# Putting the prior, the loads and the stores of a mixture-of-softmaxes kernel into one hardware queue

## The chip, the cores and the metric

The kernel runs on one core of a Trainium2 chip. The metric is the device time of one execution in microseconds (us), here always the median of several runs. A run of one core has no second die to compare with, so a run counts as slow only if it is over 1.5% above the fastest of its kernel.

## The reference

```python
logits: (32, 128, 4, 4096) float32      prior: (32, 128, 4) float32
prior_probs = softmax(prior, axis=-1)
softmax     = softmax(logits, axis=-1)
mixture     = sum over the 4 heads of prior_probs[..., None] * softmax     # (32, 128, 4096)
```

There are 4096 rows of 4 heads of 4096 values: 268.4 MB in and 67.1 MB out.

## The kernel before

A tile is 128 rows (one in each partition) with all four heads, 8.39 MB, and there are 32 tiles. Two tile buffers take the loads, two output buffers the results. For each tile ScalarE makes four exps with their sums, VectorE the reciprocals, GpSimd the four weights (the "weight multiply"), and VectorE adds up the four weighted heads in four steps. A helper, `only`, gives each instruction exactly the waits that are listed.

```python
def load(u):                       # all loads on SyncE's queue
    ...                            # cuts: whole tiles, halves for the first and the last three
    ld = nc.sync.dma_start(out=ltile[:, u % 2, h:to], in_=lg[u // J, u % J, :, h:to, :])
    if u >= 2:
        only(ld, adds[u - 2, 0] if h == 0 else exps[u - 2, to - 1])
    ...

def store(u, acc, eng, lo=0, hi=V):
    st = eng.dma_start(out=ov[u // J, u % J, :, lo:hi], in_=acc[:, lo:hi])
    stores[u] = only(st, adds[u, H - 1])
...
    load(0)
    nc.scalar.dma_start(out=pr, in_=pv)          # the prior, ScalarE's queue
    load(1)
...
        for h in range(H):
            late = h == H - 1 and 4 <= u < U - 3
            if h == H - 1 and 0 < u < U - 3:
                store(u - 1, obuf[:, (u - 1) % 2], nc.scalar)     # stores 0 to 27
            exp(h, *((stores[u - 4],) if late else ()))
            ...
        if u + 2 < U:
            load(u + 2)
        if u == U - 3:                                            # stores 28 to 31: SyncE
            store(u - 1, obuf[:, (u - 1) % 2], nc.sync)
            store(u, acc, nc.sync)
```

`late` is one more wait of a tile's fourth exp, for store u-4; the list of waits of this kernel shows no time lost to it. At the end of the build one function moves the first half of load 0 ahead of the start barrier.

The softmax here doesn't subtract the row's maximum and nothing guards it: scores larger than these inputs give would overflow.

## Time and profile before

| | before |
|---|---|
| device time | 781.02 us |
| span | 779.3 us |
| busy: VectorE, ScalarE | 67%, 60% |
| transfer engines' time, SyncE's queue + ScalarE's queue | 82.3% + 17.6% |
| moved | 335.66 MB, 431 GB/s |
| steady distance from one tile's landing to the next | 24.18 us |

The last row is taken from the starts of the first exp of each tile, which waits for the load: tile 14 at 354.86, tile 27 at 669.25, 13 tiles. The transfer engines are busy all the time, so the reading is about them. The page's table of issues tells the time from issue to landing:

```profile
out_dram<-obuf ACTq DMA_DIRECT2D x28, 2048.0 KB, 29.4
ltile<-in_logits_dram SPq DMA_DIRECT2D x28, 30.9
pr<-in_prior_dram ACTq DMA_DIRECT2D x1, 64.0 KB, 7.0
```

Its columns are tile and tensor, issuing engine, count, size (left out for the whole tiles), and the median time to landing in us. With no load beside them, stores 29 and 30 landed 4.83 and 4.85 us after the store before; beside a load a store takes 29.4, because the two take turns row by row.

### The profile page before, as it was taken

Reading aid. Unit: us, or ns where it says so; the run is one execution under the profiler, and the core shown is the slowest. Engines: PE = TensorE matmul, PEld = TensorE weight load, DVE = VectorE, ACT = ScalarE, POOL = GpSimd, SP = SyncE. Lnnn points to the kernel's source line nnn. Section 1 sums busy time; section 2 is a strip of 40 time slices with the busy share of each in tenths; the row PEclk is TensorE's granted clock in tenths of the full one; section 3 lists DMA queues with packets and bytes.
Section 4 is the critical chain, followed back from the end, with each engine's and each line's share of the span. In section 5 each row is a group of like instructions: output and inputs, shape, how many; then the busy total and the mean of one; then the engine's idle time right before and its main releaser. Section 6 shows DMA issues by size and latency. Waiting matters only on the chain.

```text
span 779.3 us, 654 instructions
## 1 busy us (share of the span) xinstructions
DVE 521.0 (67%) x174; ACT 466.7 (60%) x258; POOL 8.3 (1%) x41
## 2 busy tenths in 40 slices
DVE  4447875558755587555775557855578655689886
ACT  4476555775457755577555675546765567657782
POOL 0000000000000000000000000000000000000000
DMA  9999999999999999999999999999999999999998
GB/s 407 457 417 401 470 407 434 428 461 428 405 467 403 458 420 433 442 443 418 431 454 407 454 408 467 420 415 447 432 442 417 463 399 463 410 427 433 434 429 377
DMA packets 10117, 335.66 MB, mean 431 GB/s; under 512 B 1136, under 2 KB 1136, under 8 KB 1152
## 3 DMA queue, kind: packets, MB, share of 16 engines
q1 hardware_dynamic: 6048, 276.83, 82.3%
q10 hardware_dynamic: 4064, 58.79, 17.6%
q14 instruction: 5, 0.04, 0.0%
HBM read 268.50 MB, written 67.11 MB: 431 GB/s over the span
## 4 chain that ended last, share of the span: by engine, by line
DMA 64%; ACT 27%; DVE 6%; issue 2%; POOL 0%; DVEq 0%; POOLq 0%
DMA ltile<-in_logits_dram 62%; ACT ebuf L159 19%; ACT ltile L159 8%; DVE obuf L177 5%; DMA out_dram<-obuf 2%; DVE ltile L183 1%; POOL coeff L170 0%; DVE rden L168 0%; DVEq L240 0%; POOLq L240 0%; POOLq L170 0%
## 5 line engine op out<-in xcount | busy, mean ns | idle before, releaser
L183 DVE SCALAR_TENSOR_TENSOR obuf<-ebuf,coeff,obuf 128x4096 f32<-128x4096 f32 x90 | 403.6, 4484 | 3.8 <-POOL coeff L170 0.6
L159 ACT ACTIVATE ebuf<-ltile 128x4096 f32<-128x4096 f32 x90 | 322.9, 3589 | 7.4 <-DMA ltile<-in_logits_dram 7.4
L159 ACT ACTIVATE ltile<-ltile 128x4096 f32<-128x4096 f32 x38 | 137.3, 3614 | 280.6 <-DMA ltile<-in_logits_dram 280.6
L168 DVE RECIPROCAL rden<-dsum 128x4 f32<-128x4 f32 (+1 forms) x36 | 6.3, 175 | 227.9 <-ACT ebuf L159 225.1
L177 DVE TENSOR_SCALAR obuf<-ltile,coeff 128x4096 f32<-128x4096 f32 x30 | 70.6, 2353 | 10.2 <-POOL coeff L170 10.2
L183 DVE SCALAR_TENSOR_TENSOR ltile<-ltile,coeff 128x4096 f32<-128x4096 f32 (+1 forms) x7 | 27.0, 3875 | 0.8 <-POOL coeff L170 0.6
L159 ACT ACTIVATION_READ_ACCUMULATOR ebuf<-ltile 128x1 f32 x90 | 16.8, 186 | 0.0
L170 POOL TENSOR_TENSOR coeff<-rden,pp 128x4 f32<-128x4 f32 (+1 forms) x36 | 7.2, 200 | 755.3 <-DVE rden L168 745.4
L159 ACT ACTIVATION_READ_ACCUMULATOR ltile<-ltile 128x1 f32 x38 | 7.1, 186 | 0.0
L139 DVE TENSOR_REDUCE pmax<-pr 16x256 f32<-16x1024 f32 x1 | 1.2, 1208 | 7.8 <-DMA pr<-in_prior_dram 7.8
L141 ACT ACTIVATE pr<-pr 16x1024 f32<-16x1024 f32 x1 | 1.1, 1055 | 7.8 <-DVE pr L140 7.8
L177 DVE TENSOR_SCALAR ltile<-ltile,coeff 128x4096 f32<-128x4096 f32 x2 | 4.7, 2354 | 0.6 <-POOL coeff L170 0.6
L144 DVE TENSOR_TENSOR pn<-pr,pmax 16x1024 f32<-16x1024 f32 x1 | 1.9, 1939 | 0.1
L141 ACT ACT_TABLE_LOAD x1 | 1.3, 1283 | 1.2 <-PEq L229 1.2
L142 DVE TENSOR_REDUCE pmax<-pr 16x256 f32<-16x1024 f32 x1 | 1.2, 1207 | 1.1 <-ACT pr L141 1.1
L149 DVE STREAM_TRANSPOSE pp<-pn 32x256 f32<-32x256 f32 x4 | 1.7, 435 | 0.1
L143 DVE RECIPROCAL pmax<-pmax 16x256 f32<-16x256 f32 x1 | 1.7, 1741 | 0.0
L140 DVE TENSOR_TENSOR pr<-pr,pmax 16x1024 f32<-16x1024 f32 x1 | 1.2, 1211 | 0.0
L138 POOL MEMSET pn<- 32x1024 f32 x1 | 0.9, 941 | 0.3 <-POOLq L229 0.3
L229 POOL MEMSET const-bfloat16-1.0<- 128x1 bf16 x1 | 0.1, 106 | 0.0
L229 POOL MEMSET const-uint8-127<- 128x1 uint8 x1 | 0.1, 106 | 0.0
L229 POOL MEMSET const-float32-0.0<- 128x1 f32 x1 | 0.1, 103 | 0.2 <-issue 0.2
(1 smaller groups left out, 0.1 us busy)
## 6 DMA issues: line engine op xcount, KB each, us to landing
out_dram<-obuf ACTq DMA_DIRECT2D x28, 2048.0 KB, 29.4
ltile<-in_logits_dram SPq DMA_DIRECT2D x7, 4096.0 KB, 26.1
ltile<-in_logits_dram SPq DMA_DIRECT2D x2, 2048.0 KB, 30.9
out_dram<-obuf SPq DMA_DIRECT2D x2, 2048.0 KB, 33.9
out_dram<-ltile SPq DMA_DIRECT2D x1, 2048.0 KB, 17.2
out_dram<-ltile SPq DMA_DIRECT2D x2, 1024.0 KB, 4.8
ltile<-in_logits_dram SPq DMA_DIRECT2D x28, 30.9
pr<-in_prior_dram ACTq DMA_DIRECT2D x1, 64.0 KB, 7.0
```

Source lines behind the costliest of these rows:

```text
L139: nc.vector.reduce_max(pmax, pr, axis=AX.X)
L140: nc.vector.tensor_sub(pr, pr, pmax.unsqueeze(2).to_broadcast([G, R, H]))
L141: nc.scalar.activation(pr, pr, AF.Exp)
L142: nc.vector.reduce_sum(pmax, pr, axis=AX.X)
L143: nc.vector.reciprocal(pmax, pmax)
L144: nc.vector.tensor_mul(pn[0:G].rearrange("g h r -> g r h"), pr, pmax.unsqueeze(2).to_broadcast([G, R, H]))
L149: nc.vector.transpose(pp[32 * t : 32 * (t + 1)], pq[:, :, :, 32 * t : 32 * (t + 1)])
L159: ex = nc.scalar.activation(es[h], lt[:, h], AF.Exp, accum_out=dsum[:, u, h : h + 1])
L168: rc = nc.vector.reciprocal(rden[:, u, h : h + n], dsum[:, u, h : h + n])
L170: mul = nc.gpsimd.tensor_mul(coeff[:, u, h : h + n], rden[:, u, h : h + n], ppu[:, h : h + n])
L177: st = nc.vector.tensor_scalar(out=acc[:, lo:hi], in0=es[h][:, lo:hi], scalar1=coeff[:, u, h : h + 1], scalar2=None, op0=ALU.mult,)
L183: st = nc.vector.scalar_tensor_tensor(out=acc[:, lo:hi], in0=es[h][:, lo:hi], scalar=coeff[:, u, h : h + 1], in1=acc[:, lo:hi], op0=ALU.mu ...
```

## The change

The intent is one queue for everything: the prior first, then the loads, each store between two loads, and no issuing work on ScalarE. The core of the diff:

```diff
-def early_first_load(nc):
+def early_transfers(nc):
+    # (cut) moves the first TWO transfers of SyncE ahead of the barrier: the prior, half of load 0
...
+        nc.sync.dma_start(out=pr, in_=pv)
         load(0)
-        nc.scalar.dma_start(out=pr, in_=pv)
         load(1)
...
-                late = h == H - 1 and 4 <= u < U - 3
                 if h == H - 1 and 0 < u < U - 3:
-                    store(u - 1, obuf[:, (u - 1) % 2], nc.scalar)
-                exp(h, *((stores[u - 4],) if late else ()))
+                    store(u - 1, obuf[:, (u - 1) % 2], nc.sync)
+                exp(h)
```

More of the change, by code (lines that the diff above doesn't have):

```diff
@@ L11, with of_sp @@
 AX = mybir.AxisListType
-def early_first_load(nc):
+def early_transfers(nc):
     blocks = nc.main_func.blocks
-    first = next(
-        (b, i)
-        for b in blocks[1:]
-        for i in b.instructions
-        if i.engine == mybir.EngineType.SP and i.opcode == "DMACopy"
-    )
-    block, ins = first
-    assert not ins.sync_info.on_wait
-    block.instructions.remove(ins)
-    at = next(
-        n
-        for n, i in enumerate(blocks[0].instructions)
-        if i.engine == mybir.EngineType.SP and i.opcode == "Drain"
-    )
-    blocks[0].instructions.insert(at, ins)
+    def of_sp(block, opcode):
+        return [
+            i
+            for i in block.instructions
+            if i.engine == mybir.EngineType.SP and i.opcode == opcode
+        ]
+    body = next(b for b in blocks[1:] if of_sp(b, "DMACopy"))
+    for ins in of_sp(body, "DMACopy")[:2]:
+        assert not ins.sync_info.on_wait
+        body.instructions.remove(ins)
+        drain = of_sp(blocks[0], "Drain")[0]
+        blocks[0].instructions.insert(blocks[0].instructions.index(drain), ins)
 @with_exitstack
@@ L46 @@
     nc = tc.nc
-    nc.at_finalize(early_first_load)
+    nc.at_finalize(early_transfers)
     B, S, H, V = logits.shape
```

## The prediction

> **What bounds the kernel now.** I read the page's busy shares first, then its transfer rows, then the chain of waits, then stretches of the run one by one. The busy shares and the transfer rows:
>
> ```profile
> DVE 521.0 (67%) x174; ACT 466.7 (60%) x258; POOL 8.3 (1%) x41
> ...
> DMA  9999999999999999999999999999999999999998
> ...
> DMA packets 10117, 335.66 MB, mean 431 GB/s; under 512 B 1136, under 2 KB 1136, under 8 KB 1152
> ...
> q1 hardware_dynamic: 6048, 276.83, 82.3%
> q10 hardware_dynamic: 4064, 58.79, 17.6%
> ```
>
> No compute engine is above 67%, and the transfer engines are at 9 tenths in every slice but the last. The two hardware queues (q1 is SyncE's, q10 ScalarE's) add up to 99.9% of the 16 engines' time. So the kernel is bound by transfers: 268.4 MB of logits in, 67.1 MB out, at 431 GB/s over 779.3 us. No wait could be removed to gain much, unless the engines themselves moved bytes faster. The stretches between landings tell whether they can (columns: length, busy us of DVE, ACT, POOL with counts, granted clock, transfer share, GB/s):
>
> ```profile
> 22.39:41.73 19.34, 11.58 (x5) 7.30 (x4) 0.20 (x1) 1.00 1.00 434
> 112.34:693.42 581.08, 383.60 (x121) 348.14 (x193) 4.82 (x24) 1.00 1.00 433
> ```
>
> The first stretch lies between the landings of tiles 0 and 1. Only one queue works then (the whole-window transfer view shows q1 alone, at 100.2%), and one tile of 8.389 MB takes 19.34 us, 434 GB/s. The second is 24 steady tiles, each a load of 8.389 MB and a store of 2.097 MB on two queues: 581.08 / 24 = 24.21 us a tile, 433 GB/s. One queue of pure loads is as fast as two queues of mixed traffic. Pure stores on one queue are seen at the end: stores 28, 29 and 30 were issued on q1 at 727.84, 736.98 and 756.35 and took 36.0, 31.7 and 17.2 us to land, so they landed at 763.8, 768.7 and 773.6: 4.86 us each on average, 431 GB/s.
>
> **What the Trainium skill says.** "DMA: Bandwidth & Descriptors", section "Issuing engines are not separate DMA queues": transfers from sync, scalar and gpsimd run on the same 16 engines and interleave; issuing from several saves only sequencer time. The trace agrees: 434 with one queue, 433 with two. The same page, "Where 436 GB/s comes from", gives a fabric ceiling of 435.2 GB/s; the measured 433 to 434 is within 0.5% of it, so I expect no rate above today's. Same page, "Queues, rings and completion order": each engine round-robins between its queues packet by packet. The trace agrees. A load packet here is a row of 64 KB and a store packet 16 KB (58.79 MB in 4064 packets), so in turn-taking a store gets one byte in five: 2.097 MB at 433/5 GB/s is 24.2 us, and as stores come every 24.2 us and land 29.4 us after issue, each queues some 5 us behind the one before it. That is one store always in flight beside the loads.
>
> **The change part by part.** First, 28 stores and the prior leave ScalarE's queue. An issue took ScalarE's sequencer 0.338 us (the median of the 28), in all 28 × 0.338 = 9.5 us. That lies beside its arithmetic: in the steady part ScalarE's four exps take 14.5 us of 24.2, and it sits idle 9.66 us per tile for the load. Worth 0 on the path.
>
> Second, does SyncE, issuing in program order, ever hold a load back behind a store that isn't ready? SyncE's order becomes load(u+2), store(u), load(u+3). Load(u+2) waits for the first VectorE step of tile u, store(u) for its fourth, load(u+3) for the first of tile u+1. VectorE does these in just that order, so each wait ends in the order of issue and nothing is held back.
>
> Third, does the single queue run dry? Let T(u) be the landing of load u. From the timeline, tile 27 landed at 669.25, its first VectorE step ended at 686.67 (T+17.4, issue of load 29) and its last at 700.20 (T+31.0, issue of store 27). In one queue in order, a load takes 19.34 and a store 4.86, so the period is 24.20. After T(u+1) the engines do store(u-1) until T(u+1)+4.86 and must then find load(u+2), issued at T(u)+17.4 = T(u+1)-6.8: a margin of 11.7 us. Store(u) must be there at T(u+2) = T(u)+48.4 and is there at T(u)+31: margin 17. The output buffer is wanted when the weight multiply of tile u+2 runs, at T(u+2)+14.8, and store(u) is through at T(u+2)+4.86 plus its receipt, which the skill's same page ("Anatomy of one DMA") puts at most of 2 us: margin about 8. All margins are many times a transfer's latency. The opening is the tightest: load 3 is issued at about 59.2 and the queue has load 2 until 61.1 and store 0 until 65.9.
>
> Fourth, the sum per tile: two queues 24.21, one queue 19.34 + 4.86 = 24.20. Over the 28 tiles concerned the difference is about -0.3 us, which is zero within the 0.05 us to which I know the store's 4.86.
>
> Fifth, the opening. Today the span starts with the first half of load 0, with the prior 0.79 us later on ScalarE's queue:
>
> ```profile
> 0.00 1.62 SPq L100 DMA_DIRECT2D ltile<-in_logits_dram  x3
> 0.79 0.39 ACTq L136 DMA_DIRECT2D pr<-in_prior_dram  x1
> 7.81 1.21 DVE L139 TENSOR_REDUCE pmax<-pr 16x256 f32<-16x1024 f32 x1 [7.81 <-DMA pr<-in_prior_dram]
> 12.66 3.62 ACT L159 ACTIVATE ltile<-ltile 128x4096 f32<-128x4096 f32 x1 [1.31 <-DMA ltile<-in_logits_dram]
> ```
>
> After, SyncE issues the prior first, and the load one issue later: +0.35 us (its issues took 0.33 to 0.44). The prior's 64 KB (0.15 us at 433 GB/s) are moved in either kernel. The prior should land some 2 to 3 us into the span rather than at 7.8, and VectorE's preparation, done at about 18 today, some 5 us earlier. It is needed at 29.98 by the first weight multiply, so the gain is 0.
>
> Sixth, the end. The last stretch of the chain of waits:
>
> ```profile
> 700.23 18.06 DMA out_dram<-obuf
> ...
> 721.03 28.16 DMA ltile<-in_logits_dram
> 749.19 0.02 issue
> 749.22 7.32 ACT ltile L159 x4
> ...
> 764.29 4.50 DVE ltile L183
> ```
>
> Once the first half of tile 31 has landed at 749.22, what is left is fixed: four exps, two and two half VectorE steps, a last store of 1 MB landing in 4.8. Beside it the queue has 10.49 MB to move, 24.2 us, until 773.5, when the last half store is issued; both ends meet. Which bytes come before that landing? Today loads 0 to 30 and stores 0 to 27; stores 28 to 31 are behind load 31 on SyncE's queue already. After: the same set. So the landing moves by the opening's 0.35 us alone. The 10.0 us wait of the weight multiply for store 27 (the 18.06 line) may grow by some 3 us, as that store now stands behind both halves of load 29 (about 721 against 718.3); load 31's first half is then issued near 724.5, while load 30 keeps the queue full until about 739. Still hidden.
>
> Sum: 781.02 + 0.35 - 0.3 (zero within error) and an allowance of 0.3 for changes of direction inside one queue, from store to load, which this trace never shows: about 781.4.
>
> **The rivals.** (a) One queue has a bubble at each boundary, since the end of one transfer is not covered by another queue's packets. For it: half loads of 4.194 MB at the end land 9.72 us apart, 19.44 for a tile against 19.34 whole, so a boundary may cost 0.05 to 0.1. At 0.1 for each of 56 boundaries the time is 781.4 + 5.6 = 787, under 1%. Against it: the stores of the end at 4.86, and the load-only 19.34, both contain their boundary already. A drain of 2 us at every store would make 840; the three stores landing 4.9 and 4.8 apart speak against it, though all are of one direction. (b) Turn-taking costs something today, and long runs of one direction are faster. At the ceiling of 435.2 the 335.66 MB take 771.3 us against 775.2 at 433, so at most 4 us, 777.4. Against: the pure-load stretch has the same 434. (c) A wait takes over, as loads now land about 3 us sooner and stores go in a block behind them: ScalarE and VectorE would have to slip by over 8 us for the queue to feel it. Then a hole of a few us once or twice, 784 to 788; nothing in the trace speaks for it.
>
> **Range and chances.** The bytes and the rate stay, so the spread comes from 28 times a boundary of -0.05 to +0.1 us: 779.8 to 784.2. Two per cent is 15.6 us, or 0.56 us a tile. A gain of it would need more than the ceiling gives: 1 in 100. A loss needs a drain that only store-to-load boundaries could hide: 2 in 100.
>
> **What would show it right or wrong.** Right: q1 alone near 99.9%, loads landing 24.1 to 24.3 us apart in the steady part, stores landing about 22 us after issue instead of 29.4, ScalarE's wait for loads unchanged in total, the first exp at about 13.0, the prior landed before 4. Wrong: transfer digits below 9 in the middle of the run, a pitch off 24.2 by over 0.1, a wait of the weight multiply for a store in the steady part, or SyncE waiting on a store while the queue is empty.

## The result, and the profile after

The changed kernel took 784.39 us (784.14 to 785.78, 6 runs), against 781.02 (6 runs). The ratio is 1.0046, with an interval of 1.0033 to 1.0059. Ratios here are the mean time of one kernel's fast runs over that of the other's of the same rounds, so they are not quite the ratio of the medians. The class, within 2%, was as predicted; the time lies just above the range (784.2), and the loss of 3.4 us is clear of the noise.

The busy shares and transfer rows of the changed kernel's page:

```profile
DVE 520.9 (67%) x174; ACT 466.8 (60%) x258; POOL 8.4 (1%) x41
...
DMA  9999999999999999999999999999999999999997
...
q1 hardware_dynamic: 10112, 335.61, 99.6%
...
out_dram<-obuf SPq DMA_DIRECT2D x30, 2048.0 KB, 22.3
...
pr<-in_prior_dram SPq DMA_DIRECT2D x1, 64.0 KB, 2.0
```

Compute is as it was. One queue now does the work. Stores land 22.3 us after issue (about 22 was said), and the prior lands in 2.0 us. The share is 99.6% of a span that is 3.2 us longer, where the two queues together had 99.9%. This row is a mean over the 16 engines, and it does not say when they are idle or which of them. The stretches do (length, busy us of DVE, ACT, POOL, clock, transfer share, GB/s):

```profile
41.71:62.13 20.42, 9.92 (x4) 14.51 (x8) 0.20 (x1) 1.00 0.93 384
62.13:86.95 24.82, 20.35 (x7) 14.51 (x8) 0.20 (x1) 1.00 1.00 430
86.95:307.21 220.26, 143.20 (x46) 130.55 (x73) 1.82 (x9) 1.00 1.00 432
307.21:694.21 387.00, 255.76 (x81) 232.08 (x128) 3.24 (x16) 1.00 1.00 433
...
772.79:776.79 4.00, 3.87 (x2) 0.00 (x0) 0.00 (x0) 1.00 0.61 256
```

From landing to landing, tile 2 took 20.42 us (19.34 expected), tile 3 24.82, tiles 4 to 12 220.26 / 9 = 24.47, and tiles 13 to 28 387.00 / 16 = 24.19. So the steady pitch is what the prediction said, 24.20, and the time is lost in the first dozen tiles. The last row is the other end of the story: for 4.00 us near the end the engines were only 61% busy. The faster ones had finished all that was queued, and the last two half stores were not yet there to be moved. In the kernel before, the stretch that answers to it, up to the landing of store 30, had no such hole:

```profile
749.22:773.53 24.31, 23.24 (x9) 14.50 (x8) 0.39 (x2) 1.00 1.00 427
```

The hole is explained by a record that these views don't show. For each transfer the trace holds 16 increments of its semaphore, one from each engine that carried part of it. The Trainium skill, "DMA: Bandwidth & Descriptors", section "Why a DMA increments its semaphore by 16 and not by 1", says that the participating engines finish independently and that only the full 16 means that all data landed. Both traces agree: each transfer has 16 marks at different times, and the consumer starts some 0.02 us after the last. The first and last mark of some loads (us from the span's start, and their difference):

```
load of tile           before                    changed
1                41.32  41.71  0.39         41.20  41.69  0.49
2                64.12  64.56  0.44         61.39  62.11  0.72
3                87.69  88.13  0.43         85.61  86.93  1.32
4               111.88 112.32  0.43        109.81 111.71  1.90
5               136.06 136.51  0.44        133.99 137.01  3.02
8               208.61 209.79  1.19        206.64 210.09  3.45
12              305.33 306.49  1.16        303.36 307.19  3.83
27              668.04 669.23  1.19        666.09 670.01  3.92
31, first half  748.02 749.19  1.18        748.46 752.43  3.97
```

I call the difference the spread. The fastest engine of the changed kernel is 0.44 us late at tile 31, the slowest 3.24 us. Since the exps of tile 31 wait for the slowest, that is the loss: the chain of waits of the changed kernel ends as before, but from 752.45 in place of 749.22.

```profile
701.00 22.34 DMA out_dram<-obuf
...
726.08 26.34 DMA ltile<-in_logits_dram
752.43 0.02 issue
752.45 7.32 ACT ltile L158 x4
...
767.52 4.50 DVE ltile L182
```

All that follows 752.45 has the length it had before. The records of single packets show where engines fall behind. They give queue, size and times but not the engine; rows are put to an engine by the start of each at the end of the one before. A row of 64 KB normally took 2.418 us and a row of 16 KB 0.611, in both kernels. In the changed kernel the last row of load 2, the last before store 0 in the queue, took 3.07 to 3.72 us on all 16 engines. Such delays come again at the last rows of loads 3, 4, 5 and so on, on 11, 7, 8 and then fewer engines, by up to 1.06 us a row, and nearly fade out after tile 13. Few late rows lie elsewhere (seven by over 0.05 us from load 3 on, four of them beside packets of the instruction queue, q14), and no 16 KB row took over 0.63 us, so the delay sits on a load's last row, where a store comes next. In the kernel before, load 2's last row took 2.85 to 2.92 once, and after that only three single rows in the steady part were late, by 0.24, 0.53 and 0.25 us, each beside an 8 KB packet of q14 at 147.88, 193.96 and 511.15. Those made most of its own spread of 1.2.

### The profile page after: what moved, and what is told of

Same layout as the page of the kernel before. It is cut to its first block, busy times and chain, and to the rows that moved or that the text cites. A ratio compares the mean times of both kernels' runs of the same rounds, so it can differ in the third digit from the quotient of the medians.

```text
span 782.5 us, 680 instructions
## 1 busy us (share of the span) xinstructions
DVE 520.9 (67%) x174; ACT 466.8 (60%) x258; POOL 8.4 (1%) x41
## 3 DMA queue, kind: packets, MB, share of 16 engines
q1 hardware_dynamic: 10112, 335.61, 99.6%
## 4 chain that ended last, share of the span: by engine, by line
DMA 63%; ACT 27%; DVE 7%; issue 1%; POOL 0%; DVEq 0%; SPq 0%; POOLq 0%
DMA ltile<-in_logits_dram 60%; ACT ebuf L158 19%; ACT ltile L158 8%; DVE obuf L176 5%; DMA out_dram<-obuf 3%; DVE obuf L182 2%; DVE ltile L182 1%; POOL coeff L169 0%; DVE rden L167 0%; DVEq L238 0%; SPq L99 0%; POOLq L238 0%; POOLq L169 0%
## 6 DMA issues: line engine op xcount, KB each, us to landing
out_dram<-obuf SPq DMA_DIRECT2D x30, 2048.0 KB, 22.3
```

## The experiments

Eleven kernels ran; each number of a spread is from the one trace of its kernel. Theory 1 is that the 16 engines fall out of step where load turns to store in one queue, and that each landing waits for the slowest. Rival 1 is the opening (the moved prior), rival 2 a cost at every boundary throughout; they are not the rivals (a) to (c) of the prediction. The first four undo or move parts of the change.

**The stores alone.** The kernel before, with `nc.scalar` changed to `nc.sync` in the store, the wait `late` taken out as in the change, and the prior left where it was:

```diff
-                    store(u - 1, obuf[:, (u - 1) % 2], nc.scalar)
-                exp(h, *((stores[u - 4],) if late else ()))
+                    store(u - 1, obuf[:, (u - 1) % 2], nc.sync)
+                exp(h)
```

> The kernel before with one part of the change: the 28 stores go to SyncE's queue, each ahead of the next load; the prior stays on ScalarE's queue and the opening is that of before. Theory 1 (drift: in one queue in order the 16 transfer engines fall out of step at the first changes from load to store, and each landing then waits for the slowest): 784.4, within 0.5, and the landing of a steady load is spread over 3.5 to 4 us as in the changed kernel, against 1.2 before. Rival 1 (the moved prior and the new opening cost it): 781.0. Rival 2 (each boundary of load and store costs about 0.12 us throughout): 784.4 too, but with steady tiles 24.3 us apart all through.

Measured: 784.00 us against 780.98, ratio 1.0039 (1.0024 to 1.0054). The spread grew from 0.49 at tile 1 to 3.89 at tile 11 and was 4.00 at tile 31. Its chain of waits:

```profile
725.70 26.35 DMA ltile<-in_logits_dram
752.05 0.02 issue
752.07 7.32 ACT ltile L159 x4
```

The tile lands at 752.05, as in the changed kernel. The stores make the loss; the prior isn't needed for it. The steady pitch was 24.18 (tile 14 at 355.31, tile 27 at 669.70), so rival 2, a cost at every boundary, falls.

**The opening alone.** The changed kernel with the stores back on ScalarE's queue (the reverse of the diff above).

> The changed kernel with the 28 stores put back on ScalarE's queue: the prior first on SyncE and the new opening alone. Theory 1 and rival 2: 780.7 to 781.3, spread of the landings 1.2 us or less. Rival 1 (opening): 784.4. My prediction's own fifth step said +0.35 for this part: 781.4.

Measured: 781.48 us against 780.98, ratio 1.0006 (0.9991 to 1.0021). The spread at tile 31 was 1.15.

```profile
721.50 28.12 DMA ltile<-in_logits_dram
749.62 0.02 issue
749.64 7.32 ACT ltile L158 x4
```

The rival of the opening falls as the main cause. The half microsecond is of the size that the prediction gave the opening, but the interval includes no change at all.

**Twelve stores in one queue, then two queues.** The base is the changed kernel, here and in the next run with the wait `late` put back.

```diff
-                    store(u - 1, obuf[:, (u - 1) % 2], nc.scalar)
+                    store(u - 1, obuf[:, (u - 1) % 2], nc.sync if u <= 12 else nc.scalar)
```

> The changed kernel with stores 0 to 11 in SyncE's queue and stores 12 to 27 on ScalarE's. Theory 1 (the lag is made in the first dozen tiles and then kept to the end): 783.5 to 784.4, landings spread over 3 us or more to the end. Rival 2 (a cost at every boundary): 781.0 + 12/28 of 3.4 = 782.5. If turn-taking pulls the engines together again: below 781.8 with a spread that shrinks after tile 12.

Measured: 784.84 us (784.27 to 785.71), ratio 1.0052. The spread was 3.28 at tile 13, 3.92 at tile 14, 4.7 from tile 16 to tile 28 and 3.48 at tile 31. It rose once more, over the three tiles at the switch; two queues then neither added to it nor took it back until the half loads of the last tiles. The full loss came with 12 of the 28 stores (0.4 us more than theory 1 had said), and with the wait `late` in place, so taking that wait out isn't the cause.

**Two queues, then one.** The same line with the two engines exchanged.

> The reverse: stores 0 to 11 on ScalarE's queue, 12 to 27 in SyncE's. Theory 1 in the form that the lag is made wherever engines in step change from load to store: 783.5 to 784.4, with the spread growing from 1.2 after tile 12. Theory 1 in the form that only the opening makes it: 781.0 to 781.6, spread staying near 1.2. Rival 2: 781.0 + 16/28 of 3.4 = 782.9.

Measured: 784.13 us (783.88 to 784.85), ratio 1.0041. The spread was 1.41 at tile 13 and then 2.31, 2.91, 3.28 and 3.75 at tiles 16, 17, 18 and 20, and 3.81 at tile 31. So the lag is not a matter of the opening. It is made wherever the one queue begins, within some seven tiles.

**Halves and quarters.** Four runs changed the length of the blocks: each steady load and each store in 2 or 4 pieces by columns, in two queues (controls) or in one queue with a piece of a store after each piece of a load. The core of the edit for halves:

```diff
-            cuts = (0, H)
+            cuts = tuple(range(0, H + 1, 2))
...  # one queue, issued at the end of tile u:
+            load half a of u+2; store half b of u-1; load half b of u+2; store half a of u
```

> Control for the next run. Two queues as before (opening of the changed kernel), but each steady load is two halves (rows of 32 KB) and each store two halves (rows of 8 KB). Smaller packets cost time of their own: in the traces a 32 KB packet took 1.213 us against 2.418 for 64 KB, an 8 KB one 0.309 against 0.611 for 16 KB; per engine and tile 16 x 1.213 - 8 x 2.418 = 0.064 and 16 x 0.309 - 8 x 0.611 = 0.056, over 28 tiles 3.4 us: 784.9 (from the 781.5 of two queues with this opening), landings spread over about 1.2 us. No theory differs on this run.

> One queue in order, with half a store between each two half loads, so that a block of stores lasts some 2.4 us per engine in place of 4.9. Theory 1 with a lag that stops growing when the slowest engines are nearly one block of stores behind: spread about 1.9 us at the plateau, time about 0.7 us over the control. If the lag does not depend on the length of the block: spread 3.9, time 3 us over the control. If every boundary costs: twice the boundaries, 6 us over the control.

> Control for the next run: two queues, loads and stores in quarters (rows of 16 KB and 4 KB). Per engine and tile 32 x 0.611 - 8 x 2.418 = 0.208 and 32 x 0.159 - 8 x 0.611 = 0.200, over 28 tiles 11.4 us: about 793, spread about 1.2 us.

> One queue in order, a quarter of a store between each two quarter loads: blocks of 1.2 us per engine. Theory 1 with the plateau at one block: spread about 1 us, time equal to the control within 0.5. If the lag does not depend on the block: spread 3.9 and 3 us over the control. If every boundary costs 0.12: 10 us over it.

Measured: halves 788.58 in two queues and 785.31 in one; quarters 807.00 (3.3% slower than before) and 791.04. All four missed the times, and the controls failed as controls. With halves in two queues the stores lagged until the output buffers ran short, as the waits of that run show (who waited for whom, us in total, times, longest):

```profile
POOL coeff L171 <- DMA out_dram<-obuf: 667.8, 28, 24.7
```

With quarters it was ScalarE that waited for stores, 129.7 us in all. The queues stayed full in the middle, but the last tiles' arithmetic came late. The one-queue runs can be read against their own pitch instead. It was 24.27 for halves and 24.46 for quarters in most of the steady part. Against 24.18 that is 28 x 0.09 = 2.5 and 28 x 0.28 = 7.8 us for the shorter rows. Their spreads at tile 31 were 2.62 and 3.60, that is 1.5 and 2.5 us above the 1.15 of two queues. From 781.48 this gives 785.5 and 791.8 (measured 785.31 and 791.04), so pitch and spread together account for the times within a microsecond. The rule, a plateau of nearly one block, had said about 1.9 us for halves and 1 for quarters. Halves ended at 2.62, a little over their block of 2.5. The quarters are no clean test: their spread rose by 0.44, 0.64 and 0.61 us beside three packets of the instruction queue (at 159.15, 403.85 and 648.48), so 1.7 of the 3.60 us is not a matter of turns. The other 1.9 is still above the 1 that was said, so the rule is not shown.

**Loads in the place of the stores.** Wrong results on purpose: the output of tiles 0 to 27 is never written.

```diff
+        if u < U - 4:
+            st = eng.dma_start(out=acc, in_=lg[u // J, u % J, :, 0, :])
+        else:
             st = eng.dma_start(out=ov[u // J, u % J, :, lo:hi], in_=acc[:, lo:hi])
```

> Wrong results on purpose: in the changed kernel each of the 28 stores is replaced by a load of the same size and row length (128 rows of 16 KB from the logits) into the same output buffer, in the same place of SyncE's queue with the same waits. Sizes, order, boundaries and buffers stay; the queue no longer changes direction. If the change of direction from load to store makes the engines lag: landings spread over 1.3 us or less to the end, 781.0 to 781.8 (what two queues took with this opening is 781.5). If alternating long and short transfers in one queue is enough: spread near 3.9 and 784.4.

Measured: 782.70 us against 781.02, ratio 1.0022 (1.0006 to 1.0039). The spread was 0.45 at tile 4 and 1.09 at tile 16, 1.47 at tile 31, and its steps come with single late rows on one engine, each beside a packet of the instruction queue (137.77, 191.10, 484.45); no last row of a load was late by 0.05 us.

```profile
out_dram<-obuf SPq DMA_DIRECT2D x2, 2048.0 KB, 35.8
...
obuf<-in_logits_dram SPq DMA_DIRECT2D x28, 2048.0 KB, 22.4
...
724.36 26.40 DMA ltile<-in_logits_dram
750.76 0.02 issue
750.78 7.32 ACT ltile L161 x4
```

Same sizes, order, waits and buffers, but no turn from load to store, and the lag is gone. The run takes away the stores as such together with the turn; that it is the turn follows only with the late rows above, which stand right before a store. The time missed my figure by 0.9 us. The pitch was 24.25 against 24.18 (tile 14 at 352.56, tile 27 at 668.17: 24.28 with a step of 0.35 in it), some 27 x 0.07 = 1.9 us in all (rows took 2.422 and 0.614 us in place of 2.418 and 0.611), partly offset by a shorter opening: tile 2 landed at 61.01 here, and at 62.13 in the changed kernel.

**The changed kernel again.**

> The changed kernel once more, for how far its lag repeats: 784.0 to 784.8, the spread of the landings 3.7 to 4.1 us by tile 14, made in tiles 2 to 11 as in the first trace.

Measured: 784.81 us (784.53 to 785.64), ratio 1.0050. The spread was 3.30 at tile 9, 3.66 at tile 14 and 3.70 at tile 31. The lag repeats, a little more slowly made; time and spread miss by 0.01 and 0.04 us.

**A later issue of the loads.**

```diff
-                only(ld, adds[u - 2, 0] if h == 0 else exps[u - 2, to - 1])
+                only(ld, adds[u - 2, 1 if u < U - 4 else 0] if h == 0 else exps[u - 2, to - 1])
```

> The changed kernel with each load of tiles 2 to 29 issued one VectorE step (4.5 us) later, which leaves the queue some 7 us of work at each issue. In the traces the delayed packets lie within a few us of such an issue. If the issue of the next load delays them, the lag should be made elsewhere and differ: a spread off 3.9 by over 1 us and a time off 784.4 by over 0.8. If it is the boundary of load and store: 784.4 within 0.5, spread 3.6 to 4.1, delayed packets still the last ones of a load.

Measured: 784.57 us against 781.02, ratio 1.0046 (1.0031 to 1.0061), spread 3.50 at tile 31, 0.1 us outside what I had written. The late rows were again the last ones of loads. Of 64 that were late by over 0.05 us, 36 had ended before the nearest issue of a load, 27 were under way at it and one began after it; in the changed kernel 65 of 81 began after it and 16 were under way. The issue is not what delays them.

No experiment beat the kernel before, which stays the best.

## Why the prediction was right or wrong

- **The bound and the rate were right.** The transfers bound both kernels, and the steady pitch in one queue was 24.19 us against 24.20 worked out. So rival (b), a gain from long runs of one direction, did not come.
- **No wait of SyncE, no dry queue: right.** The transfer digits stay at 9 but for the last, and the weight multiply waited for a store only once, for store 27: 14.2 us against 10.0, with the store landing at 723.34 (about 721 was said). It was hidden, as said. ScalarE's wait for loads, which was to stay as it was, grew from 288.0 to 296.9 us; its 9.5 us of issuing had gone.
- **The opening: right in size as far as the noise lets tell, wrong in its reason.** The first half tile landed no later (its exp started at 12.63 against 12.66, 13.0 was said), although its issue came 0.44 us into the span. With the opening alone, the kernel was 0.5 us slower, and the trace puts it in tile 2: 23.44 us from landing to landing against 22.85. Why is open.
- **The end was right in kind.** The last chain follows the landing of tile 31's first half, and all after it has its old length. The prediction moved that landing by the opening's 0.35 us; it moved by 3.24.
- **The step that failed is the fourth, the sum per tile, with the allowance** that the sum adds for it: "0.3 for changes of direction inside one queue, from store to load". The direction that hurt was the other one, from load to store, and the stores alone cost 784.00 - 780.98 = 3.0 us, ten times the 0.3. The working treated 16 engines as one: with bytes and rate the same, the landing had to come at the same time. But a landing is the last of 16, and the engines came apart. The rows that were late from load 2 to tile 28 add up to 2.1 us an engine on average in the changed kernel and 0.6 before, that is 1.5 us more on average (the mean of the 16 marks at tile 31 moved by 1.54), while the slowest engine, for which the landing waits, was 3.24 us late at tile 31.
- **Rival (a) named the place and had the wrong law.** I weighed a bubble at each of 56 boundaries and argued against it from the stretches of pure loads and pure stores. Those have no turn from load to store, and without it the run with loads in place of stores had no lag. The loss isn't one per boundary either: it stops growing after some 5 to 12 tiles, whenever these come.
- **The range was narrower than its own rivals.** It took 28 boundaries at -0.05 to +0.1 us (from 781.4 that gives 780.0, not 779.8, at its low end), where rival (a) counted 56; with 56 it would have reached 787 and held the measured time, but by luck. Rival (c)'s 784 to 788 holds it by luck too: the queue did not run dry until the last two half stores.

What is shown: the stores in SyncE's queue make the loss; it lies in a spread between engines that grows within some 5 to 12 tiles and then stays; it needs the turn from load to store; the issue of the next load doesn't make it. What stays open: why the last row before a store is delayed at all, why turn-taking of two queues, which turns after every row, doesn't delay it, and what stops the lag near 4 us. In the two-queue kernel the last row of a load is followed by a store's row before the load's completion mark, in one queue by that mark and then the store; whether this is the reason was only argued, not tried.

## What to carry to other kernels

When a kernel is bound by transfers at the ceiling, look beyond the mean of the 16 engines: a landing is that of the slowest, and here a lag made in the first tiles was paid once, at the end. In a kernel like this one, leave stores on a second queue beside the stream of loads unless the issuing engine is short of time; one queue took 9.5 us of issuing off ScalarE, which had been hidden, and the kernel lost 3.4 us. Evidence from stretches of pure loads and pure stores says nothing about the turns between them.

## What the Trainium skill lacked or had wrong

- "DMA: Bandwidth & Descriptors", "Rules for kernel authors", says that spreading transfers over SP, ACT and GpSimd doesn't help bandwidth and only saves issue time. As to the rate that holds here (24.18 us a tile in two queues, 24.19 in one). As to the time it doesn't quite: stores in a queue of their own made the kernel 3.0 us faster than stores in the queue of the loads (780.98 against 784.00).
- The same page, "Why a DMA increments its semaphore by 16 and not by 1", says that the engines finish independently, and its section on the iDMA fabric, within an explanation that it calls unconfirmed, that a bulk load runs at the pace of its slowest engine; neither says how far apart engines get. Here the first and last of 16 were 0.4 to 1.8 us apart in the kernel before and up to 4.0 in the changed one.
- No page that I looked up (DMA, HBM, trace analysis) speaks of a cost of turning from load to store within one queue. Here single 64 KB rows before a store took up to 3.72 us in place of 2.418 while the engines were in step, and 2.42 later.
- "Runtime: NRT & Kernel Launch", "Instruction fetch mechanics", calls the fetch through a transfer queue mostly hidden. It doesn't say that the fetch takes one engine's time from the kernel's own transfers: three rows in the kernel before were late by 0.24 to 0.53 us beside 8 KB packets of the instruction queue, and the spread stayed larger after the first two.
- The table "Measured" in the section "Bandwidth" of "DMA: Bandwidth & Descriptors" is for transfers from GpSimd and ends at 425 GB/s for 16 MB; it has no row for SyncE, where an 8.39 MB load ran at 434 here.
